# A hybrid encoder step: the first RMSNorm's weights move into PSUM, its inputs go first in the queue, and GpSimd's first work is placed behind the 1/sqrt chain

## The chip, the cores and the metric

The kernel runs on one core of a Trainium2 chip. The time is device microseconds (us) of one execution; lower is better. The engines are TensorE (PE; its weight loads are listed apart as PEld), VectorE (DVE), ScalarE (ACT), GpSimd (POOL) and SyncE (SP), which issues most of the DMAs. SBUF is the on-chip working memory, PSUM the memory that TensorE writes, in banks of 128 partitions by 512 fp32 columns.

## The reference

One step of a one-layer encoder over 592 tokens (16 learned meta tokens, 512 prompt tokens, 64 sample tokens), width 1024, all in fp32. Only the beginning matters here:

```
def _rmsnorm(x, w):
    xf = x.astype(jnp.float32)
    y = xf * lax.rsqrt(jnp.mean(xf * xf, axis=-1, keepdims=True) + EPS)
    return (y * w.astype(jnp.float32)).astype(x.dtype)
...
    h = _rmsnorm(x, p["norm1"])
    proj = h @ p["w_in"]
```

`proj` is 9232 columns wide. What follows it is differential attention, a gated delta rule with a causal convolution, a gated merge, and a squared-ReLU MLP of hidden width 4096.

## The kernel before

TensorE multiplies in a reduced-precision fp32 format (fp32r), so every operand is split into a high and a low part and each product is three matmuls: high by high, low by high, high by low. The normed tokens `h` are kept transposed, features on partitions, as `hh` (high) and `hl` (low), 128 x 8 x 592. The projection weights stream in tasks of 256 columns. Each raw half (`wr_d`, 512 KB) is cast by ACT to `wh_d` and its rest is `wl_d`, for the first task always on POOL.

Python code writes all engines' instructions down in one fixed order. Two parts take turns: `begin`, which makes `hh` and `hl`, and the generator `main` (from `stream`), which loads and splits weights and issues the projection matmuls `pg_d`. Each `next(main)` in `begin` lets `main` go one step: first the loads of the first task's weights, then their split, then eight matmuls at a time.

`begin` works on five token tiles (80, 128, 128, 128, 128 rows), tokens on partitions. SP loads them as `x_s` (`load_x`), and loads `norm1` repeated over all 128 partitions as `n_bc`. For a tile t:

- `square(t)`: ACT squares the row and sums it (`jk`, a READ_ACCUMULATOR follows). For tiles 0 to 2 POOL meanwhile makes `xn` = x times `n_bc`.
- `rsqrt`: nine tiny DVE instructions (`rsv`, `rsy`, `rst`, 128 x 3) give 1/sqrt for tiles 0 to 2 at once, and later, 128 x 2, for tiles 3 and 4.
- `scale(t)`: DVE multiplies by it (tiles 3 and 4: by it and by `n_bc`).
- `turn(t)`: TensorE transposes `xn` in two halves of four 128-column blocks into PSUM banks `pxt`; ACT casts each half to `hh`, and DVE subtracts to give `hl` (both in `split`).

The projection's columns are worked in two parts: tokens 0 to 335, which need tiles 0 to 2, and tokens 336 to 591, which need tiles 3 and 4 too. Five PSUM banks are shared by everything that asks `bank` for one.

DVE, ACT, POOL and TensorE each take their instructions strictly in this written order.

Of the kernel before, what the change touches and what calls it, by code (L numbers as in the profile page):

```python
# [208 lines left out]
def stream_step_kernel(  # L209
# [243 lines left out]

    def load_x(pl, t, nm):
        xt = pl.tile([P, D], F32, name=f"x_{nm}{t}", tag="xt")
        if t == 0:
            Q.dma_start(xt[0:16], meta)
            Q.dma_start(xt[16:80], x_prompt[0, 0:64])
        elif t < 4:
            Q.dma_start(xt, x_prompt[0, 128 * t - 64:128 * t + 64])  # L460
        else:
            Q.dma_start(xt[0:64], x_prompt[0, 448:512])
            Q.dma_start(xt[64:128], x_sample[0])
        return xt

    def begin(sp):

        n1_bc = sp.tile([P, D], F32, name="n1_bc", tag="n1")
        ss = sp.tile([P, NT], F32, name="ss", tag="ss")
        v1 = sp.tile([P, P], F32, name="v1", tag="v1")  # L470
        v2 = sp.tile([P, P], F32, name="v2", tag="v2")
        V.memset(ss, 1.0)
        S.activation(ss[:, 4:5], ss[:, 4:5], AF.Square)
        xts = [load_x(sp, t, "s") for t in range(2)]
        Q.dma_start(n1_bc, flat(norm1, 0, [[0, P], [1, D]]))
        Q.dma_start(ident, consts[:, 0:P])
# [9 lines left out]
        Q.dma_start(v2[74:75].rearrange("o (a d) -> o a d", a=2), flat(q_norm, 0, [[64, 1], [0, 2], [1, 64]]))  # L486
        Q.dma_start(cst[:, P:3 * P], consts[:, P:3 * P])
        xns = {}

        def square(t):  # L490
            n = TILES[t][1]
            jk = sp.tile([P, D], F32, name=f"jk{t}", tag="jk")
            S.activation(jk[:n], xts[t][:n], AF.Square, accum_out=ss[:n, t:t + 1])
            xns[t] = sp.tile([P, D], F32, name=f"xn{t}", tag="xn")
            if t < 3:
                G.tensor_tensor(xns[t][:n], xts[t][:n], n1_bc[:n], ALU.mult)

        def scale(t, r):
            n = TILES[t][1]
            if t < 3:  # L500
                V.tensor_scalar(xns[t][:n], xns[t][:n], r[:n], None, ALU.mult)
            else:
                V.scalar_tensor_tensor(xns[t][:n], xts[t][:n], r[:n], n1_bc[:n], ALU.mult, ALU.mult)

        def turn(t):
            c0, n = TILES[t]
            for q in range(2):
                pv = bank(f"pxt{t}{q}").rearrange("p (k c) -> p k c", k=4)
                for k in range(4):
                    TE.transpose(pv[:, k, :n], xns[t][:n, (4 * q + k) * P:(4 * q + k + 1) * P], ident[:n, :n])  # L510
                split(hh[:, 4 * q:4 * q + 4, c0:c0 + n], hl[:, 4 * q:4 * q + 4, c0:c0 + n], pv[:, :, :n])

        for t in range(3):
            square(t)
        r = rsqrt(sp, ss[:, 0:3], 3, 1.0 / D, EPS)
        for t in range(3):
            scale(t, r[:, t:t + 1])
        next(main)
        square(3)
        turn(0)  # L520
        turn(1)
# [29 lines left out]
    def prepare(sp):  # L551
# [1013 lines left out]
```

## Time and profile before

| | |
|---|---|
| runs of the kernel before | 1348.81 us median of 3 (1346.97 to 1351.1) |
| the profiled execution | 1348.32 us, of which the profile's span is 1346.5 us |
| TensorE busy | 1297.8 us (96% of the span) |
| VectorE busy | 694.0 us (52%) |
| ScalarE busy | 564.5 us (42%) |
| GpSimd busy | 264.7 us (20%) |
| mean granted TensorE clock | 0.994 |

The times in the trace count from the start of the span. A busy share is over the whole span; the stretch of interest is its first 40 us, where the shares are quite different.

### The profile page before, as it was taken

The numbers are of one execution on the slowest core, as the hardware profiler recorded it, in microseconds if no ns is written. First come the engines' busy times: TensorE is split into PE (matmuls) and PEld (weight loads), VectorE is DVE, ScalarE is ACT, GpSimd is POOL, SyncE is SP. The second block draws the span as 40 slices with busy tenths as digits, with TensorE's granted clock in tenths as the row PEclk, the third lists the DMA queues.
The fourth block names the chain that finished last, engine by engine and source line by source line (L and its number), as shares of the span: only waits on it lengthen the run. The fifth ranks groups of instructions, "written<-read, shape, count | busy, mean of one in ns | idle before, by whom it ended". The sixth has DMA issues, their size and how long they took to land.

```text
span 1346.5 us, 25748 instructions
## 1 busy us (share of the span) xinstructions
PE 1297.8 (96%) x10365; PEld 1260.4 (94%) x10365; DVE 694.0 (52%) x1547; ACT 564.5 (42%) x1354; POOL 264.7 (20%) x283
## 2 busy tenths in 40 slices
PE   2999999999999999999899999999999999999998
PEld 2998899999899999998788899999999999999998
DVE  5766899533457624448877844445333233233232
ACT  3556544343563343346676723233431431431421
POOL 5101412200132000062524102100410410310300
PEclk9999999999999999999999899999999999999999
DMA  6313343532644422685644256622223223222231
GB/s 174 90 53 116 100 124 113 169 91 72 196 135 127 141 78 66 189 242 162 198 141 135 94 203 226 204 78 80 79 79 95 76 82 94 67 92 86 72 112 53
DMA packets 163947, 161.07 MB, mean 120 GB/s; under 512 B 23546, under 2 KB 143628, under 8 KB 163828
## 3 DMA queue, kind: packets, MB, share of 16 engines
q1 hardware_dynamic: 162372, 155.99, 38.2%
q0 software_dynamic: 1456, 3.44, 0.9%
q8 instruction: 81, 1.33, 0.4%
q14 instruction: 38, 0.31, 0.1%
HBM read 124.46 MB, written 37.88 MB: 121 GB/s over the span
## 4 chain that ended last, share of the span: by engine, by line
PE 46%; DVE 3%; DMA 1%; ACT 1%; issue 0%; SPq 0%; DVEq 0%; ACTq 0%
PE pg_dn L164 15%; PE pg_u L164 15%; PE pg_o L164 4%; PE pg_bb L164 4%; PE pg_ba L164 3%; PE pg_g L164 1%; DVE sc L164 1%; PE ppo L164 1%; DVE mx L164 1%; PE psc L164 1%; PE pwT L164 1%; ACT sc L164 0%; DMA thb<-th_d 0%; PE pxr L164 0%; PE pyo L164 0%
## 5 line engine op out<-in xcount | busy, mean ns | idle before, releaser
L164 PE MATMUL pg_dn<-uh,wh_dn 128*128 128x288 f32 x512 | 151.6, 296 | 0.0
L164 PE MATMUL pg_dn<-ul,wh_dn 128*128 128x288 f32 x512 | 151.6, 296 | 0.0
L164 PE MATMUL pg_u<-h2h,wh_u 128*128 128x288 f32 x512 | 151.4, 296 | 0.0
L164 PE MATMUL pg_u<-h2h,wl_u 128*128 128x288 f32 x512 | 151.2, 295 | 0.0
L164 PE MATMUL pg_u<-h2l,wh_u 128*128 128x288 f32 x512 | 151.2, 295 | 0.0
L164 PE MATMUL pg_dn<-uh,wl_dn 128*128 128x288 f32 x512 | 151.1, 295 | 0.0
L164 PE MATMUL pg_a<-wh_a,hh 128*128 128x256 f32 (+1 forms) x480 | 136.3, 284 | 2.0 <-ACT sq L164 2.0
L164 PE MATMUL pg_a<-wh_a,hl 128*128 128x256 f32 (+1 forms) x480 | 136.3, 284 | 0.0
L164 PE MATMUL pg_a<-wl_a,hh 128*128 128x256 f32 (+1 forms) x480 | 135.4, 282 | 0.0
L164 PE MATMUL pg_d<-hl,wh_d 128*128 128x336 f32 (+1 forms) x384 | 116.1, 302 | 0.6 <-DVE hl L164 0.6
L164 PE MATMUL pg_d<-hh,wh_d 128*128 128x336 f32 (+1 forms) x384 | 116.0, 302 | 0.6 <-ACT hh L164 0.6
L164 PE MATMUL pg_d<-hh,wl_d 128*128 128x336 f32 (+1 forms) x384 | 115.8, 302 | 0.0
L164 POOL TENSOR_TENSOR wl_u<-wr_u,wh_u 128x1024 fp32r<-128x1024 f32 x22 | 52.9, 2402 | 260.5 <-ACT wh_u L164 260.5
L164 DVE TENSOR_TENSOR x<-x,pg_dn 128x288 f32<-128x288 f32 x64 | 29.1, 454 | 132.5 <-PE pg_dn L164 132.5
L164 PEld LDWEIGHTS pg_u<-h2h,wh_u 128*128 128x128 f32 x512 | 96.5, 189 | 0.1
L164 PEld LDWEIGHTS pg_u<-h2l,wh_u 128*128 128x128 f32 x512 | 96.5, 189 | 0.0
L164 PEld LDWEIGHTS pg_u<-h2h,wl_u 128*128 128x128 f32 x512 | 96.4, 188 | 0.0
L164 PEld LDWEIGHTS pg_dn<-uh,wl_dn 128*128 128x128 f32 x512 | 96.3, 188 | 0.0
L164 PEld LDWEIGHTS pg_dn<-ul,wh_dn 128*128 128x128 f32 x512 | 96.1, 188 | 0.0
L164 PEld LDWEIGHTS pg_dn<-uh,wh_dn 128*128 128x128 f32 x512 | 96.1, 188 | 0.0
L164 PEld LDWEIGHTS pg_a<-wh_a,hh 128*128 128x128 f32 (+1 forms) x480 | 86.5, 180 | 3.1 <-ACT sq L164 2.5
L164 PEld LDWEIGHTS pg_a<-wh_a,hl 128*128 128x128 f32 (+1 forms) x480 | 86.7, 181 | 0.7 <-issue 0.6
(371 smaller groups left out, 3536.6 us busy)
## 6 DMA issues: line engine op xcount, KB each, us to landing
wr_u<-in_w_up_dram SPq DMA_DIRECT2D x32, 512.0 KB, 3.6
wr_dn<-in_w_down_dram SPq DMA_DIRECT2D x32, 512.0 KB, 3.5
wr_d<-in_w_in_dram SPq DMA_DIRECT2D x24, 512.0 KB, 3.9
wr_a<-in_w_in_dram SPq DMA_DIRECT2D x24, 512.0 KB, 4.1
wr_g<-in_w_in_dram SPq DMA_DIRECT2D x16, 512.0 KB, 5.5
at_d<-st SPq DMA_DIRECT2D x48, 128.0 KB, 2.2
th_d<-gt SPq DMA_DIRECT2D x16, 288.0 KB, 2.2
wr_z<-in_w_in_dram SPq DMA_DIRECT2D x8, 512.0 KB, 3.8
```

The costliest lines, as they stand in the source:

```text
L164: r = f(*a, **kw)
```

## The change

All of it lies in `begin` and in one line of `prepare`.

- `norm1` is loaded as one row of 1024 and spread over the partitions by two matmuls of a row of ones with it, into two PSUM banks (`pn10`, `pn11`; `pn` in a profile). These banks stay taken until the last `scale`.
- Tokens go first in SP's queue: tiles 0, 1, 2, then the row, then the identity.
- POOL's multiplications by `norm1` are gone. `scale` does both products in DVE, in two instructions of 512 columns, for all five tiles.
- POOL's first instruction now is a tiny copy that reads the result of the 1/sqrt chain. The split of the first weights (`wl_d`) is queued behind it.
- `turn` leaves the `hl` subtractions to a new function `lower`, which `begin` calls after the next tile's `scale`. Tile 3's squares on ACT move behind the casts of tile 2, and tiles 3 and 4 are transposed after 24 and 32 matmuls.
- The ones come from a DVE memset at the start, not from POOL's in `prepare`.

```diff
-    def load_x(pl, t, nm):
+    def load_x(pl, t):
...
-        n1_bc = sp.tile([P, D], F32, name="n1_bc", tag="n1")
+        n1 = sp.tile([1, D], F32, name="n1", tag="n1")
...
+        xts = [load_x(sp, t) for t in range(3)]
+        Q.dma_start(n1, norm1)
+        Q.dma_start(ident, consts[:, 0:P])
         V.memset(ss, 1.0)
+        V.memset(onesr.bitcast(F32), 1.0)
         S.activation(ss[:, 4:5], ss[:, 4:5], AF.Square)
-        xts = [load_x(sp, t, "s") for t in range(2)]
-        Q.dma_start(n1_bc, flat(norm1, 0, [[0, P], [1, D]]))
-        Q.dma_start(ident, consts[:, 0:P])
-        xts.append(load_x(sp, 2, "s"))
         next(main)
...
+        n1_bc = [bank(f"pn1{q}") for q in range(2)]
+        for q in range(2):
+            TE.matmul(n1_bc[q], onesr.bitcast(F32)[0:1, :], n1[:, 512 * q:512 * q + 512], start=True, stop=True)
...
-            xns[t] = sp.tile([P, D], F32, name=f"xn{t}", tag="xn")
-            if t < 3:
-                G.tensor_tensor(xns[t][:n], xts[t][:n], n1_bc[:n], ALU.mult)
 
         def scale(t, r):
             n = TILES[t][1]
-            if t < 3:
-                V.tensor_scalar(xns[t][:n], xns[t][:n], r[:n], None, ALU.mult)
-            else:
-                V.scalar_tensor_tensor(xns[t][:n], xts[t][:n], r[:n], n1_bc[:n], ALU.mult, ALU.mult)
+            xns[t] = sp.tile([P, D], F32, name=f"xn{t}", tag="xn")
+            for q in range(2):
+                cs = slice(512 * q, 512 * q + 512)
+                V.scalar_tensor_tensor(xns[t][:n, cs], xts[t][:n, cs], r[:n], n1_bc[q][:n], ALU.mult, ALU.mult)
...
-                split(hh[:, 4 * q:4 * q + 4, c0:c0 + n], hl[:, 4 * q:4 * q + 4, c0:c0 + n], pv[:, :, :n])
+                hi, lo = (x[:, 4 * q:4 * q + 4, c0:c0 + n] for x in (hh, hl))
+                S.copy(hi, pv[:, :, :n])
+                rest.append((lo, pv[:, :, :n], hi.bitcast(F32)))
+            return rest
+
+        def lower(rest):
+            for lo, pv, hi in rest:
+                V.tensor_tensor(lo, pv, hi, ALU.subtract)
...
-        for t in range(3):
-            scale(t, r[:, t:t + 1])
+
+        G.tensor_scalar(ss[:, 0:3], r, 1.0, 0.0, ALU.mult, ALU.add)
         next(main)
+        scale(0, r[:, 0:1])
+        rest = turn(0)
+        scale(1, r[:, 1:2])
+        lower(rest)
+        rest = turn(1)
+        scale(2, r[:, 2:3])
+        lower(rest)
+        rest = turn(2)
         square(3)
-        turn(0)
-        turn(1)
         square(4)
-        turn(2)
+        lower(rest)
...
-            if i in (3, 5):
-                turn(3 if i == 3 else 4)
+            if i in (2, 3):
+                lower(turn(i + 1))
...
-        G.memset(onesr.bitcast(F32), 1.0)
```

GpSimd's queue from its first instruction on, before (`xn` is the product with `norm1`, `wl_d` the low part of the first weights):

```order
L164 TENSOR_TENSOR xn0_196<-x_s0_168,n1_bc_162 80x1024
L164 TENSOR_TENSOR xn1_200<-x_s1_171,n1_bc_162 128x1024
L164 TENSOR_TENSOR xn2_204<-x_s2_175,n1_bc_162 128x1024
L164 TENSOR_TENSOR wl_d010_222<-wr_d0100_177,wh_d010_221 128x1024
L164 TENSOR_TENSOR wl_d010_222<-wr_d0104_179,wh_d010_221 128x1024
L164 DMA ba_r_382<-in_w_in_dram 128x8x16
```

and with the change:

```order
L164 TENSOR_SCALAR ss_163<-rsy3_207 128x3
L164 TENSOR_TENSOR wl_d010_219<-wr_d0100_178,wh_d010_218 128x1024
L164 TENSOR_TENSOR wl_d010_219<-wr_d0104_180,wh_d010_218 128x1024
L164 DMA ba_r_390<-in_w_in_dram 128x8x16
```

The three products are gone, and the two weight splits stand behind an instruction that needs `rsy`, the last result of the 1/sqrt chain.

VectorE's queue from the end of that chain on, before (`hl` the low part of the transposed tokens, its last operand the cast `hh`):

```order
L164 SCALAR_TENSOR_TENSOR rsy3_208<-rst2_207,rsy3_208 128x3
L164 TENSOR_SCALAR xn0_196<-xn0_196,rsy3_208 80x1024
L164 TENSOR_SCALAR xn1_200<-xn1_200,rsy3_208 128x1024
L164 TENSOR_SCALAR xn2_204<-xn2_204,rsy3_208 128x1024
L164 TENSOR_TENSOR hl_158<-pxt00_230,hh_157 128x4x80
```

and with the change, up to the first subtraction that the second matmul needs:

```order
L164 SCALAR_TENSOR_TENSOR xn0_224<-x_s0_166,rsy3_207,pn10_195 80x512
L164 SCALAR_TENSOR_TENSOR xn0_224<-x_s0_166,rsy3_207,pn11_196 80x512
L164 SCALAR_TENSOR_TENSOR xn1_239<-x_s1_169,rsy3_207,pn10_195 128x512
L164 SCALAR_TENSOR_TENSOR xn1_239<-x_s1_169,rsy3_207,pn11_196 128x512
L164 TENSOR_TENSOR hl_158<-pxt00_227,hh_157 128x4x80
L164 TENSOR_TENSOR hl_158<-pxt01_233,hh_157 128x4x80
L164 SCALAR_TENSOR_TENSOR xn2_256<-x_s2_171,rsy3_207,pn10_195 128x512
L164 SCALAR_TENSOR_TENSOR xn2_256<-x_s2_171,rsy3_207,pn11_196 128x512
L164 TENSOR_TENSOR hl_158<-pxt10_244,hh_157 128x4x128
L164 TENSOR_TENSOR hl_158<-pxt11_250,hh_157 128x4x128
L164 TENSOR_TENSOR hl_158<-pxt20_261,hh_157 128x4x128
```

Tile 2 is now scaled behind tile 0's two subtractions, and tile 2's own first subtraction stands behind tile 1's.

On TensorE, where tile 3 is transposed, before (the 32nd matmul stands ahead of it; `pg_d01010` is the second output of the first task):

```order
L164 MATMUL pg_d01010_318<-hl_158,wh_d010_221 128x336
L164 MATMUL pxt30_327<-cst_74,xn3_229 128x128 x4
L164 MATMUL pxt31_334<-cst_74,xn3_229 128x128 x4
L164 MATMUL pg_d01010_318<-hh_157,wl_d010_222 128x336
```

and with the change (the 24th matmul ahead of it, and tile 4 eight matmuls later):

```order
L164 MATMUL pg_d01000_283<-hh_157,wl_d010_219 128x336
L164 MATMUL pxt30_326<-cst_74,xn3_304 128x128 x4
L164 MATMUL pxt31_332<-cst_74,xn3_304 128x128 x4
L164 MATMUL pg_d01010_340<-hh_157,wh_d010_218 128x336
```

Tile 3's transposes moved forward past eight matmuls. From the second column part on, the order on all five engines is the one of before, row for row, except for tile numbers.

## Rows read from the trace of the kernel before

**Rows 1.** The page, part 1: busy time by engine.
```profile
PE 1297.8 (96%) x10365; PEld 1260.4 (94%) x10365; DVE 694.0 (52%) x1547; ACT 564.5 (42%) x1354; POOL 264.7 (20%) x283
```

**Rows 2.** Waits of TensorE: us in total, times, longest.
```profile
PE pxt L164 <- DVE xn L164: 22.7, 1, 22.7
...
PE pkn L164 <- DVE ktok L164: 2.5, 1, 2.5
```

**Rows 3.** Timeline of ScalarE, 0 to 40 us: start, duration, what, [idle before].
```profile
10.73 1.06 ACT L164 ACTIVATE jk<-x_s 128x1024 f32<-128x1024 f32 x1 [3.49 <-DMA x_s<-in_x_prompt_dram]
...
12.13 1.04 ACT L164 CAST wh_d<-wr_d 128x1024 fp32r<-128x1024 f32 x1 [0.25 <-DMA wr_d<-in_w_in_dram]
14.70 1.05 ACT L164 CAST wh_d<-wr_d 128x1024 fp32r<-128x1024 f32 x1 [1.53 <-DMA wr_d<-in_w_in_dram]
...
27.33 1.06 ACT L164 CAST hh<-pxt 128x512 fp32r<-128x512 f32 x2
```

**Rows 4.** Timeline of VectorE, 8 to 31 us.
```profile
11.91 2.08 DVE L164 TENSOR_SCALAR rsv<-ss 128x3 f32<-128x3 f32 x1 [11.04 <-ACT jk L164]
...
18.62 2.21 DVE L164 TENSOR_TENSOR rst<-rst,rsy 128x3 f32<-128x3 f32 x1
...
21.91 2.08 DVE L164 TENSOR_SCALAR xn<-xn,rsy 80x1024 f32<-80x1024 f32 x3
24.01 1.02 DVE L164 TENSOR_TENSOR hl<-pxt,hh 128x320 fp32r<-128x320 f32 x2
...
27.93 1.29 DVE L164 TENSOR_TENSOR hl<-pxt,hh 128x512 fp32r<-128x512 f32 x2 [0.83 <-ACT hh L164]
29.14 0.16 DVE L164 TENSOR_SCALAR rsv<-ss 128x2 f32<-128x2 f32 x1
...
30.71 0.16 DVE L164 SCALAR_TENSOR_TENSOR rsy<-rst,rsy 128x2 f32<-128x2 f32 x1
```

**Rows 5.** Timeline of GpSimd, its first work.
```profile
9.27 6.94 POOL L164 TENSOR_TENSOR xn<-x_s,n_bc 80x1024 f32<-80x1024 f32 x3 [8.82 <-DMA n_bc<-in_norm_dram]
16.17 4.64 POOL L164 TENSOR_TENSOR wl_d<-wr_d,wh_d 128x1024 fp32r<-128x1024 f32 x2
```

**Rows 6.** Timeline of TensorE, 22 to 40 us.
```profile
22.72 4.66 PE L164 MATMUL pxt<-cst,xn 80*128 80x80 f32 x24 [22.72 <-DVE xn L164]
27.95 0.42 PE L164 MATMUL pg_d<-hh,wh_d 128*128 128x336 f32 x1 [0.57 <-ACT hh L164]
28.68 0.42 PE L164 MATMUL pg_d<-hl,wh_d 128*128 128x336 f32 x1 [0.31 <-DVE hl L164]
...
33.56 1.04 PE L164 MATMUL pxt<-cst,xn 128*128 128x128 f32 x8
...
38.17 0.39 PE L164 MATMUL pg_d<-hh,wh_d 128*128 128x256 f32 x1
38.90 0.39 PE L164 MATMUL pg_d<-hl,wh_d 128*128 128x256 f32 x1 [0.34 <-DVE hl L164]
```

**Rows 7.** A GpSimd tensor_tensor in the timeline at 622.66 us.
```profile
622.66 2.39 POOL L164 TENSOR_TENSOR wl_g<-wr_g,wh_g 128x1024 fp32r<-128x1024 f32 x1
```

**Rows 8.** Groups by shape, VectorE, 622.6 to 625.2, then 400 to 800: busy us, mean ns.
```profile
L164 DVE SCALAR_TENSOR_TENSOR aqT<-ptq,vec,aqT 128x464 fp32r<-128x464 f32 x1 | 0.7, 700 | 2.5 <-ACT aqT L164 2.5
...
L164 DVE SCALAR_TENSOR_TENSOR aqT<-ptq,vec,aqT 128x464 fp32r<-128x464 f32 x8 | 5.6, 696 | 5.8 <-ACT aqT L164 5.8
```

**Rows 9.** Timeline of TensorE, 105 to 112 us.
```profile
105.32 0.82 PE L164 MATMUL pk<-cst,kT 128*128 128x128 f32 x4 [1.35 <-DVE ktok L164]
...
108.22 0.48 PE L164 MATMUL pg_d<-hh,wh_d 128*128 128x336 f32 x1
108.50 0.48 PE L164 MATMUL pg_d<-hl,wh_d 128*128 128x336 f32 x1
...
111.52 0.77 PE L164 MATMUL pbv<-oh,rb 32*8 32x360 f32 x2
```

**Rows 10.** Busy us by engine in a stretch, then granted clock, DMA share, GB/s.
```profile
105.60:109.10 3.50, 3.44 (x16) 3.05 (x15) 1.68 (x3) 3.25 (x21) 0.00 (x0) 0.51 0.32 114
```

More of the change, by code (lines that the diff above doesn't have):

```diff
@@ L452, in stream_step_kernel @@
     ob = [x[:, :, 0:TQ] for x in (hh, hl)]
-    def load_x(pl, t, nm):
-        xt = pl.tile([P, D], F32, name=f"x_{nm}{t}", tag="xt")
+    def load_x(pl, t):
+        xt = pl.tile([P, D], F32, name=f"x_s{t}", tag="xt")
         if t == 0:
@@ L471, in begin @@
         v2 = sp.tile([P, P], F32, name="v2", tag="v2")
+        xts = [load_x(sp, t) for t in range(3)]
+        Q.dma_start(n1, norm1)
+        Q.dma_start(ident, consts[:, 0:P])
         V.memset(ss, 1.0)
+        V.memset(onesr.bitcast(F32), 1.0)
         S.activation(ss[:, 4:5], ss[:, 4:5], AF.Square)
-        xts = [load_x(sp, t, "s") for t in range(2)]
-        Q.dma_start(n1_bc, flat(norm1, 0, [[0, P], [1, D]]))
-        Q.dma_start(ident, consts[:, 0:P])
-        xts.append(load_x(sp, 2, "s"))
         next(main)
-        xts += [load_x(sp, t, "s") for t in range(3, NT)]
+        xts += [load_x(sp, t) for t in range(3, NT)]
         Q.dma_start(v1[0:96], conv_w[0].rearrange("w (c p) -> (w c) p", p=P))
@@ L493, in square @@
             S.activation(jk[:n], xts[t][:n], AF.Square, accum_out=ss[:n, t:t + 1])
-            xns[t] = sp.tile([P, D], F32, name=f"xn{t}", tag="xn")
-            if t < 3:
-                G.tensor_tensor(xns[t][:n], xts[t][:n], n1_bc[:n], ALU.mult)
         def scale(t, r):
             n = TILES[t][1]
-            if t < 3:
-                V.tensor_scalar(xns[t][:n], xns[t][:n], r[:n], None, ALU.mult)
-            else:
-                V.scalar_tensor_tensor(xns[t][:n], xts[t][:n], r[:n], n1_bc[:n], ALU.mult, ALU.mult)
+            xns[t] = sp.tile([P, D], F32, name=f"xn{t}", tag="xn")
+            for q in range(2):
+                cs = slice(512 * q, 512 * q + 512)
+                V.scalar_tensor_tensor(xns[t][:n, cs], xts[t][:n, cs], r[:n], n1_bc[q][:n], ALU.mult, ALU.mult)
         def turn(t):
             c0, n = TILES[t]
+            rest = []
             for q in range(2):
@@ L527, in begin @@
                 r = rsqrt(sp, ss[:, 3:5], 2, 1.0 / D, EPS)
-                for t in range(2):
-                    scale(3 + t, r[:, t:t + 1])
-            if i in (3, 5):
-                turn(3 if i == 3 else 4)
+                scale(3, r[:, 0:1])
+                scale(4, r[:, 1:2])
+            if i in (2, 3):
+                lower(turn(i + 1))
         ps = bank("pv1")
```

## The prediction

> **What bounds the kernel now.** First the busy times: TensorE is busy 96% of the span [rows 1], so only its idle time and its own work can be removed. Its list of waits comes second: the longest by far, 22.7 us, is the one before the first transposes, for `xn` [rows 2]; every later one is at most 2.5 us. So I read the first 40 us engine by engine. There the reader should follow one chain. Tile 2's square starts at 10.73, when its tokens have landed [rows 3]; the 1/sqrt chain starts at 11.91 and its last instruction is over only just before `scale` starts at 21.91 [rows 4]. Nine instructions take ten us. The same nine for tiles 3 and 4 run from 29.14 to 30.87 (30.71 and 0.16), 1.73 us [rows 4]. The difference is in the first four, which take 2.08 to 2.26 us (the first and the fourth are shown), though they handle three columns. GpSimd's five instructions run without a gap from 9.27 to 20.81 [rows 5], 2.3 us each, the length of the slow DVE rows; the fourth slow row ends at 20.83, with GpSimd's last. I read it as DVE waiting for one GpSimd instruction each time.
>
> Behind it come `scale`, 24 transposes, casts and subtractions; the first projection matmul starts at 27.95, the second, which needs `hl`, at 28.68 [rows 6]. From there TensorE nearly streams.
>
> **The change step by step.** I time the new beginning on the scale of the trace.
>
> *Tokens.* Tile 2 takes the queue place of the repeated `norm1`, which had landed when POOL began at 9.27 [rows 5]. I put tile 2 at 9.2. It could be as late as 10.73, where it is now, or as early as 8.1: 512 KB fewer are ahead of it, and such a piece takes 1.4 to 2.6 us (10.73 to 12.13, 12.13 to 14.70 [rows 3]). From its square to the chain's start passes 1.18 us (10.73 to 11.91), so the chain runs from 10.4 to 12.1 if no GpSimd instruction stands against it: 1.73 us instead of 9.9. POOL has none to run until the chain ends.
>
> *norm1 in PSUM.* Not seen in the trace. Nearest is an fp32 matmul with 360 columns, whose two records take 0.77 us [rows 9]. For 512 columns that is 1.1 us, so 2.2 for both matmuls at full clock and 4.4 at half. With the row landing by 9.0 the second bank is ready between 11.2 and 13.4; `scale` wants it at 12.8, the first at 12.1. It costs 0 to 0.6 us, and I take 0.1; the cover is the 1/sqrt chain, and each us that the row lands later costs up to one us.
>
> *Scale.* Two DVE instructions a tile. The nearest row has the same three operands (PSUM, a scalar per partition, SBUF) with 464 columns: 0.70 us [rows 8]; back to back, 512-column instructions reading PSUM come every 0.645 (1.29 for two [rows 4]). I take 0.66, so 1.32 a tile, where before it was 0.69 (2.08 for three). This is 1.9 us more on DVE for three tiles.
>
> *The weights' casts.* ACT casts the second half of the first weights before it casts any `hh`. That half landed at 14.70 [rows 3]. With 512 KB less ahead, 1.4 to 2.6 us as above, I take 1.4: 13.3, and the cast is over at 14.35. Ends: 12.1 and 14.7.
>
> *The chain to the second matmul.* Tiles 0 and 1 are scaled by 12.1 + 2.64 = 14.74. The first `hh` cast takes 0.48 from 14.35, so the first subtraction starts at about 14.86. Then DVE alone sets the pace, in the order that the listing above shows: tile 0's subtractions 1.02, tile 2's scale 1.32, tile 1's subtractions 1.25, tile 2's first 0.69 [rows 4]: 19.14. The second matmul starts at 19.2, against 28.68: 9.5 us earlier. The transposes and casts between lie beside this. Three banks are left to `pxt`, so tile 1's second half waits for tile 0's first subtraction and tile 2's second half for tile 1's; at half clock (24 transposes in 4.66, so 0.8 for four [rows 6]) the last one ends near 18.8, before it is needed.
>
> *The weights' low part.* POOL starts at 12.2 instead of 16.17, and needs 4.64 [rows 5]: by 17.0, as the second cast allows it to start at 14.4. Cover 2.2 us.
>
> *Tile 3's new place, a new wait.* TensorE reaches its transposes after 24 matmuls. From 28.68 to 33.56 there are 31 steps, 0.157 us each [rows 6]; 23 more of them end at 22.8. But ACT now squares tiles 3 and 4 after the casts of tile 2 (those end near 19.5): 2 x 1.15 us, then the chain 1.73, then half a scale 0.70: 24.3. TensorE waits 1.5 us. What stands behind it: the 24 remaining matmuls of the part and tile 4. From the transposes to the second column part it was 33.56 to 38.17, 4.61 us with 16 matmuls; with 24 it is 5.87, so 30.2, and 0.2 to 0.4 for the second half of the scale and the next matmul: 30.6 against 38.90, where the trace also had a wait for `hl` [rows 6]. That `hl` is over by 29.5 now. **Gain there: 38.9 - 30.6 = 8.3 us.**
>
> From here all queues hold the same rows as before. The later waits of TensorE are for DVE and ACT work that itself follows matmuls, so they move along. With the 0.1 for `norm1` I keep 8.2 us. The profiled execution took 1348.32 us, so 1340.1; the median of the runs shown stands 0.5 higher, and I predict 1340.4. About 0.3% (4 us) is what a measurement of this kernel can tell from no change, as its three runs lie 4.1 apart.
>
> **The rivals.**
>
> *TensorE stays at half clock.* Now its work before the first projection matmul is 24 transposes in one go, at 0.19 us each against 0.13 later [rows 6], and the matmuls behind run at full pace; after the change the transposes come in bursts of four with waits between, and the 1.5 us wait follows. The half level looks like [rows 10]: granted 0.51 (1.2 GHz) from 105.6 to 109.1, matmuls 0.28 apart [rows 9]. If the first 24 matmuls ran so, they would take 24 x 0.12 = 2.9 us more, of which the wait at tile 3 hides 1.5; or the wait itself brings on one such stretch, 3.5 us at half, 1.7 lost. Gain 6.5 to 6.8: 1341.7. For it: the fall at 105.6 came right after a wait of 1.35 us [rows 9]. Against: the clock did not fall at 28, after 0.57 and 0.31 us [rows 6], and the 1.5 us wait is a single one. Chance 0.16.
> The Trainium skill speaks for this rival: in "TensorE: Matmul & The Clock Gate", section "HAM oscillation — how this bites in real kernels", it says that work in bursts with waits between them lets the array fall back to the low clock. By it the time would be this rival's 1341.7, by the rows at 28 us my own; the 3.5 us at 0.51 show that the fall exists here.
>
> *GpSimd blocks the new scales too.* If DVE's `scale` waited for the two `wl_d` instructions as the tiny ones did, tile 1's first half would be scaled only at 17.0; then 0.66 + 1.02 + 1.32 + 1.25 + 0.69 follow: 22.0 instead of 19.2. Gain 5.4: 1342.9. For it: the rows at 11.91 to 20.83. Against: while a GpSimd tensor_tensor ran from 622.66 to 625.05 [rows 7], the instruction with a PSUM operand, a scalar and an SBUF operand took 700 ns, against 696 in the mean of all eight [rows 8]. Chance 0.07.
>
> *The slow rows had another cause* (ACT, the DMAs of that time), so the chain still takes 9.9 us from 10.4. Then `scale` starts at 20.3, the second matmul at 27.2, and the wait at tile 3 takes back the 1.5: no change, 1348. Against: the slow rows end with GpSimd's last one to 0.02 us. Chance 0.03.
>
> *The gain is given back*, most likely where TensorE waits 2.5 us for `ktok` [rows 2]: if that wait were set by a transfer that starts at a fixed time, it would grow by what was gained. It is a DVE result, so against it. 1345 to 1348. Chance 0.06.
>
> *norm1's row lands late, and the kernel is slower.* It is a single small row behind 1.3 MB of tokens. Every us after about 9 delays both banks, `scale` and all behind it by one us. From a landing at 17.3 on the gain is gone, and past 21.3 the kernel is slower by over 0.3%: 1352.5 and more. Against: what stood in about the same place had landed at 9.27 [rows 5]. Chance 0.03.
>
> **How the numbers follow.** The forecast has the remaining 0.65. Its own bounds: tile 2 and the weights at their early ends give one us more, and at their late ends (10.73 and 14.70) 1.4 to 1.5 less (both start the same chain, so they don't add up); with the scatter of the runs 1338 to 1342.5. The range takes in the half clock and the blocked scales, 1337.5 to 1344.5; the last three rivals, 0.12, lie outside. Faster by over 0.3%: 0.65 + 0.16 + 0.07 = 0.88. Within 0.3%: 0.09. Slower: 0.03.
>
> **What would show it.** Right: nine DVE rows of 0.16 us, from about 10.4 to 12.1; tile 2's square at about 9.2; `scale` rows of 0.7 with GpSimd's `wl_d` beside them; the second cast of weights at 13.3; the second `pg_d` matmul near 19.2; a wait of about 1.5 us before tile 3's transposes; the first 256-column matmuls near 30.5, and later waits as long as now. Wrong: any `scale` row of over 2 us, a wait of `scale` for `pn`, projection matmuls 0.28 apart before 30 us, or waits after 40 us whose sum is some us greater than now.

## The result, and the profile after

The changed kernel takes 1337.43 us (median of 8 runs, 1334.18 to 1345.09), the kernel before beside it 1347.67 (8 runs, 1344.41 to 1352.61): ratio 0.9939, 95% interval 0.9920 to 0.9958, or 8.2 us less (the ratio is not that of the two medians, which lie 10.2 us apart). In a second set of runs it took 1338.32 us (8 runs), ratio 0.9949 (0.9927 to 0.9971). The forecast was 8.2 us less; applied to the 1348.81 of the runs that it had, the ratio gives 1340.6 beside 1340.4. The median itself lies 0.07 us under the range's low end; the eight runs of before have a median 1.1 us below that of the three shown, too.

The timeline of the profiled execution of the changed kernel, 7 to 30 us: VectorE, ScalarE, GpSimd, then TensorE (start, duration, engine, what, [idle before]).

```profile
9.68 0.17 DVE L164 TENSOR_SCALAR rsv<-ss 128x3 f32<-128x3 f32 x1 [8.65 <-ACT jk L164]
...
11.27 0.16 DVE L164 SCALAR_TENSOR_TENSOR rsy<-rst,rsy 128x3 f32<-128x3 f32 x1
11.54 2.72 DVE L164 SCALAR_TENSOR_TENSOR xn<-x_s,rsy,pn 80x512 f32<-80x512 f32 x4
14.18 0.88 DVE L164 TENSOR_TENSOR hl<-pxt,hh 128x320 fp32r<-128x320 f32 x2
14.98 1.39 DVE L164 SCALAR_TENSOR_TENSOR xn<-x_s,rsy,pn 128x512 f32<-128x512 f32 x2
16.29 2.00 DVE L164 TENSOR_TENSOR hl<-pxt,hh 128x512 fp32r<-128x512 f32 x3
...
8.50 1.06 ACT L164 ACTIVATE jk<-x_s 128x1024 f32<-128x1024 f32 x1 [1.26 <-DMA x_s<-in_x_prompt_dram]
...
11.68 1.05 ACT L164 CAST wh_d<-wr_d 128x1024 fp32r<-128x1024 f32 x1 [0.50 <-DMA wr_d<-in_w_in_dram]
...
11.61 0.20 POOL L164 TENSOR_SCALAR ss<-rsy 128x3 f32<-128x3 f32 x1 [11.16 <-DVE rsy L164]
11.77 4.69 POOL L164 TENSOR_TENSOR wl_d<-wr_d,wh_d 128x1024 fp32r<-128x1024 f32 x2
...
7.47 3.75 PE L164 MATMUL pn<-n,onesr 1*128 1x512 f32 x4 [7.47 <-DMA n<-in_norm_dram]
12.34 5.80 PE L164 MATMUL pxt<-cst,xn 80*128 80x80 f32 x24 [1.13 <-DVE xn L164]
17.80 0.63 PE L164 MATMUL pg_d<-hh,wh_d 128*128 128x336 f32 x1
18.35 0.65 PE L164 MATMUL pg_d<-hl,wh_d 128*128 128x336 f32 x1
18.79 0.48 PE L164 MATMUL pg_d<-hh,wl_d 128*128 128x336 f32 x1
...
19.60 0.32 PE L164 MATMUL pg_d<-hh,wl_d 128*128 128x336 f32 x1
...
23.56 1.29 PE L164 MATMUL pxt<-cst,xn 128*128 128x128 f32 x8 [0.87 <-DVE xn L164]
...
29.39 0.36 PE L164 MATMUL pg_d<-hh,wh_d 128*128 128x256 f32 x1
29.59 0.28 PE L164 MATMUL pg_d<-hl,wh_d 128*128 128x256 f32 x1
```

The chain's nine rows, of which the first and the last are shown, last 0.16 to 0.17 us each and end at 11.43; before, four of them took over 2 us [rows 4]. `wl_d` runs beside four `scale` rows that come 0.66 apart. From 11.54 to 18.29 the VectorE rows follow each other without a gap, and the second `pg_d` matmul starts at their end: 18.35, against 28.68 [rows 6]. The first five `pg_d` matmuls are still 0.28 apart, the half level that [rows 9, 10] show; from 19.6 on they come at 0.155. The second column part starts at 29.39, 8.8 us earlier, and its second matmul, without the old wait for `hl`, at 29.59, 9.3 us earlier.

What happens to these 9.3 us later is seen at three waits of TensorE, and in two of the stretches at half clock of that execution (busy us of TensorE, its weight loads, DVE, ACT, POOL with counts; then granted clock, DMA share, GB/s).

```profile
95.90 0.66 PE L164 MATMUL pk<-cst,kT 128*128 128x128 f32 x4 [1.35 <-DVE ktok L164]
...
132.62 0.50 PE L164 MATMUL pkn<-cst,ktok 80*128 80x80 f32 x4 [0.67 <-DVE ktok L164]
...
573.85 0.39 PE L164 MATMUL pg_a<-wh_a,hh 128*128 128x256 f32 x1 [1.23 <-ACT sq L164]
...
466.70:480.30 13.60, 13.60 (x114) 12.86 (x113) 0.98 (x2) 3.57 (x7) 0.00 (x0) 0.50 0.06 23
651.00:654.40 3.40, 3.40 (x18) 3.38 (x17) 2.06 (x10) 1.42 (x4) 0.16 (x1) 0.50 0.11 38
```

Two of these lines in the kernel before:

```profile
145.18 0.50 PE L164 MATMUL pkn<-cst,ktok 80*128 80x80 f32 x4 [2.48 <-DVE ktok L164]
...
581.74 0.39 PE L164 MATMUL pg_a<-wh_a,hh 128*128 128x256 f32 x1 [1.97 <-ACT sq L164]
```

At 95.90 the kernel is 9.4 us ahead of before [rows 9], and at the longest wait that before had behind its beginning, for `ktok` at 145.18, it is 12.6 us ahead, since that wait is 0.67 us instead of 2.48. At 573.85 it is 7.9 ahead, after 13.6 us at half clock where before had two stretches of 3.4 us (at 105.67 and 146.63). This execution, 1345.09 us, was the longest of the eight; its mean granted clock was 0.990, that of the three shortest 0.996 and 0.997. The waits of TensorE behind 40 us add up to some 20 us before, 21 in this execution and 17 in the one profiled the second time. The table sets the same marks beside each other for all kernels that ran; the wait for `ktok` is the one of the `pk` matmuls, the times are medians, the ratios stand against the runs of before on the same chip.

| kernel | first `scale` | 2nd `pg_d` | wait for `ktok` ends | time | ratio (95%) |
|---|---|---|---|---|---|
| before | 21.91 | 28.68 | 105.32 | 1347.67 | |
| changed | 11.54 | 18.35 | 95.90 | 1337.43 | 0.9939 (0.9920 to 0.9958) |
| changed, second time | 11.46 | 18.26 | 95.58 | 1338.32 | 0.9949 (0.9927 to 0.9971) |
| tokens first alone | 19.05 | 27.73 | 105.76 | 1346.78 | 1.0003 (0.9977 to 1.0029) |
| GpSimd kept busy | 17.24 | 24.05 | 101.58 | 1343.80 | 0.9976 (0.9964 to 0.9988) |
| `norm1` in SBUF | 11.06 | 21.18 | 98.57 | 1338.72 | 0.9954 (0.9932 to 0.9976) |
| no hold | 11.16 | 17.96 | 95.06 | 1337.77 | 0.9928 (0.9913 to 0.9942) |
| old order | 11.60 | 20.72 | 98.83 | 1338.42 | 0.9946 (0.9928 to 0.9964) |
| later turns | 11.30 | 18.10 | 95.74 | 1335.29 | 0.9925 (0.9902 to 0.9947) |
| early products | 11.83 | 18.24 | 94.08 | 1335.48 | 0.9927 (0.9903 to 0.9950) |
| early products, again | 10.67 | 16.96 | 92.93 | 1333.63 | 0.9908 (0.9887 to 0.9929) |
| early products, no hold | 11.34 | 19.73 | 96.01 | 1336.95 | 0.9933 (0.9913 to 0.9953) |
| later turns, dummies | 14.05 | 23.29 | 99.26 | 1340.87 | 0.9961 (0.9945 to 0.9977) |
| early products, dummies | 12.93 | 24.35 | 100.35 | 1341.39 | 0.9960 (0.9943 to 0.9978) |

The marks differ by some tenths from one execution to the next, the times by several us; the verdicts below rest on the marks, and on a time only where the interval allows it.

The record also has each run's span and mean granted clock. Their product is an estimate of the span at full clock throughout, which counts half of a stretch at half clock as lost; it scatters by up to 2 us (one standard deviation), the times by up to 5. By it the changed kernel of the second set is 10.3 us ahead of the 17 runs of before beside it (1327.9 against 1338.2), and in the same way later turns are 10.7 ahead, early products 12.0 and 11.4, no hold 8.8, early products without the hold 8.7, the old order 7.5, `norm1` in SBUF 6.9 and GpSimd kept busy 2.5, while tokens first alone are 0.4 behind. The granted clock itself was lower in the changed kernel, 0.9938 and 0.9931 in the mean of its two sets, than in the runs of before beside the second, 0.9958.

### The profile page after: what moved, and what is told of

It reads as the page before. It is cut to its first block, busy times and chain, and to the rows that moved or that the text cites. A ratio compares the mean times of both kernels' runs of the same rounds, so it can differ in the third digit from the quotient of the medians.

```text
span 1343.3 us, 25764 instructions
## 1 busy us (share of the span) xinstructions
PE 1307.8 (97%) x10369; PEld 1265.8 (94%) x10369; DVE 688.4 (51%) x1553; ACT 564.3 (42%) x1354; POOL 256.3 (19%) x280
## 4 chain that ended last, share of the span: by engine, by line
PE 84%; DVE 6%; DMA 5%; ACT 3%; issue 2%; SPq 1%; POOL 0%; DVEq 0%; ACTq 0%; POOLq 0%
PE pg_dn L164 15%; PE pg_u L164 15%; PE pg_a L164 10%; PE pg_d L164 8%; PE pg_g L164 6%; PE pg_z L164 4%; PE pg_ba L164 4%; PE pg_o L164 4%; PE pg_bb L164 4%; DVE sc L164 2%; DMA bias_d<-bv_d 2%; PE ppo L164 2%; PE po L164 1%; DVE mx L164 1%; PE psc L164 1%
```

## The experiments

### Is it GpSimd that made the chain slow?

**Tokens first alone.** The kernel before with one edit:

```diff
-        xts = [load_x(sp, t, "s") for t in range(2)]
+        xts = [load_x(sp, t, "s") for t in range(3)]
         Q.dma_start(n1_bc, flat(norm1, 0, [[0, P], [1, D]]))
         Q.dma_start(ident, consts[:, 0:P])
-        xts.append(load_x(sp, 2, "s"))
```

> The kernel before with one part of the change alone: tile 2's tokens go ahead of the repeated norm1 and the identity in SP's queue. GpSimd keeps its three products with norm1. Theory (GpSimd blocks the chain): tile 2's square is about 1.5 to 2 us earlier (8.5 to 9.3 instead of 10.73), but the products start when norm1 has landed, at 9.5 to 11, and run seven us, so that four or more of the chain's rows still take 2.1 to 2.3 us; the second pg_d matmul is at 27 to 29 against 28.68; total within 1.5 us of before. Rival (the gain of the change comes from the earlier tokens): the chain is short or starts early enough that the second matmul comes at 19 to 25, and the total falls by 4 us or more.

Its timeline, VectorE and GpSimd:

```profile
9.48 0.16 DVE L164 SCALAR_TENSOR_TENSOR rst<-rst 128x3 f32<-128x3 f32 x1
9.67 2.36 DVE L164 SCALAR_TENSOR_TENSOR rsy<-rst,rsy 128x3 f32<-128x3 f32 x1
12.07 2.27 DVE L164 SCALAR_TENSOR_TENSOR rst<-rsy,rsv 128x3 f32<-128x3 f32 x1
14.38 2.27 DVE L164 TENSOR_TENSOR rst<-rst,rsy 128x3 f32<-128x3 f32 x1
...
19.05 3.99 DVE L164 TENSOR_SCALAR xn<-xn,rsy 80x1024 f32<-80x1024 f32 x3
...
9.63 6.94 POOL L164 TENSOR_TENSOR xn<-x_s,n_bc 80x1024 f32<-80x1024 f32 x3 [9.18 <-DMA n_bc<-in_norm_dram]
```

This is the plainest view of the cause: five rows run at 0.16 to 0.17 before GpSimd starts at 9.63, and from the first that starts behind it on every row takes one GpSimd instruction (6.94 / 3 = 2.3 us). Tokens that are 3.2 us earlier (square at 7.50 instead of 10.73) win 0.95 us at the second matmul and nothing in the time.

**GpSimd kept busy.** The changed kernel, plus six products that nothing uses:

```diff
         xns = {}
+        spare = [sp.tile([P, D], F32, name=f"sq{t}", tag="spare") for t in range(1)][0]
...
             S.activation(jk[:n], xts[t][:n], AF.Square, accum_out=ss[:n, t:t + 1])
+            for _ in range((1, 1, 4, 0, 0)[t]):
+                G.tensor_tensor(spare[:n], xts[t][:n], xts[t][:n], ALU.mult)
```

> The changed kernel with one thing added that nothing uses: six products x times x of 1024 columns on GpSimd (tiles 0, 1 and four times 2, into a spare tile), ahead of its hold, so that GpSimd runs tensor_tensors from about 5 to 19 us as it did before, while tokens, norm1 in PSUM and all else stay as changed. Theory: the 1/sqrt chain again has about four rows of 2.1 to 2.3 us, ends at 18 to 20.5 instead of 11.43, and the second pg_d matmul is at 25 to 27.5 instead of 18.35: most of the 8.2 us gain is gone. Rival (the gain came from the order of the loads or from norm1 in PSUM): nine rows of 0.17, the chain ends at 11.4 to 12, the second matmul at 18.3 to 19.5, total within 1.5 us of the changed kernel (wl_d later, which the second matmul does not need).

```profile
10.85 0.17 DVE L164 TENSOR_SCALAR rsy<-rsv 128x3 int32<-128x3 int32 x1
11.06 1.73 DVE L164 SCALAR_TENSOR_TENSOR rst<-rsy,rsv 128x3 f32<-128x3 f32 x1
12.83 0.16 DVE L164 TENSOR_TENSOR rst<-rst,rsy 128x3 f32<-128x3 f32 x1
13.02 1.74 DVE L164 SCALAR_TENSOR_TENSOR rst<-rst 128x3 f32<-128x3 f32 x1
...
4.97 11.75 POOL L164 TENSOR_TENSOR sq<-x_s 80x1024 f32<-80x1024 f32 x6 [4.52 <-DMA x_s<-in_x_prompt_dram]
```

In this timeline (VectorE, then GpSimd) the slow rows are back with the tokens, `norm1` and the order as changed: four of 1.19 to 1.74 us. The second matmul is at 24.05, 5.7 us later than in the changed kernel, and its median is 6.0 us above that of the kernel named no hold below, which has the changed kernel's marks, on the same chip. I had expected 25 to 27.5: the GpSimd instructions took less than 2 us here (1.89 each, six in 11.75), and two rows of the chain, not one, passed per instruction. These instructions stand 0.08 us apart, those of the kernel before overlap by 0.04; whether that is why was not tried.

### What the place of norm1, the hold and the order are worth

**`norm1` in SBUF.** The changed kernel with these lines, and without the two matmuls:

```diff
-        n1 = sp.tile([1, D], F32, name="n1", tag="n1")
+        n1 = sp.tile([P, D], F32, name="n1", tag="n1")
...
-        Q.dma_start(n1, norm1)
+        Q.dma_start(n1, flat(norm1, 0, [[0, P], [1, D]]))
...
+        n1_bc = [n1[:, 512 * q:512 * q + 512] for q in range(2)]
```

> The changed kernel with norm1 not in PSUM: the DMA repeats it over the partitions of an SBUF tile at the same queue place (512 KB instead of 4 KB), `scale` reads x and norm1 both from SBUF, and the two norm1 matmuls are gone; the hold stays. Theory (blocking by GpSimd depends on where DVE's operands lie): `scale` rows now stand against the two wl_d (2.4 us each): one or two of the `scale` rows take 2 us or more instead of 0.73, or wl_d's own rows become longer, and the second pg_d matmul is at 20.5 to 22 instead of 18.35; total 2 to 3.5 us slower. Rival (PSUM does not matter for `scale`, only the chain's tiny rows were blocked): `scale` rows stay at 0.66 to 0.75, and the one cost is that norm1 and the weights land later by 1.2 to 2.6 us; `scale` starts as norm1 lands, the second matmul is at 18.3 to 20; total 0 to 1.5 us slower.

Timeline of VectorE and GpSimd:

```profile
11.06 2.74 DVE L164 SCALAR_TENSOR_TENSOR xn<-x_s,rsy,n 80x512 f32<-80x512 f32 x4
14.24 0.89 DVE L164 TENSOR_TENSOR hl<-pxt,hh 128x320 fp32r<-128x320 f32 x2 [0.44 <-ACT hh L164]
15.05 4.27 DVE L164 SCALAR_TENSOR_TENSOR xn<-x_s,rsy,n 128x512 f32<-128x512 f32 x2
...
12.48 6.29 POOL L164 TENSOR_TENSOR wl_d<-wr_d,wh_d 128x1024 fp32r<-128x1024 f32 x2 [0.53 <-ACT wh_d L164]
```

Tile 2's two rows take 4.27 us (1.52 and 2.83) instead of 1.39, and the two `wl_d` 6.29 instead of 4.69: the first one had started while tile 1's rows ran, and was itself held up. The second matmul moves from 18.35 to 21.18, as the theory had it. The rival, a later landing, falls: tile 2's rows start at 15.05, against 14.98, so the loss is in the rows themselves. The time is less plain: the ratio is 0.9954 against 0.9928 for no hold on the same chip, 3.5 us with intervals that overlap, while the medians lie 1.0 apart and the estimates at full clock 1.8. So PSUM is what lets `scale` run beside GpSimd.

**No hold.** The changed kernel without its line `G.tensor_scalar(ss[:, 0:3], r, 1.0, 0.0, ALU.mult, ALU.add)`.

> The changed kernel without GpSimd's tiny first instruction, so that its two wl_d may start as soon as the first cast of the weights is over (11.18 us in the trace of the changed kernel), while the 1/sqrt chain runs from 9.68 to 11.43. Theory (a DVE instruction with all operands in SBUF waits for the GpSimd tensor_tensor that is running): the last one or two rows of the chain take up to 2.3 us instead of 0.17, `scale` starts at 13 to 16 instead of 11.54, and the second pg_d matmul is at 19.8 to 22.5 instead of 18.35; total 1.5 to 4 us slower. Rival (the slow rows had another cause, and the hold does nothing): nine rows of 0.17, `scale` at 11.5, the second matmul at 18.3 to 18.5, no difference in time.

The rival's numbers came, though not for its reason: `wl_d` waits for the first cast of the weights and starts at 10.88, and of the chain only the last row, at 10.89, was still to come. It took 0.16, although a row that started 0.04 us behind a GpSimd instruction took 2.36 in tokens first alone; why this one escaped is not shown. Behind it `scale` has its PSUM operand. Here the hold is worth nothing (from the first `scale` to the second matmul pass 6.8 us with and without it); the landing of the weights holds GpSimd as long. Where that cover is gone, it is worth something, as early products without the hold shows in the next part.

**Old order.** The changed kernel with the instructions behind the chain in the order of before, the subtractions back in `turn`:

```diff
+        for t in range(3):
+            scale(t, r[:, t:t + 1])
+        square(3)
+        turn(0)
+        turn(1)
+        square(4)
+        turn(2)
...
-            if i in (2, 3):
-                lower(turn(i + 1))
+            if i in (3, 5):
+                turn(3 if i == 3 else 4)
```

> The changed kernel with one part undone: the order of the kernel before for DVE, ACT and TensorE behind the chain (all three `scale`, tile 3's square, then the transposes of tiles 0, 1 and 2 each with its casts and subtractions, tile 4's square ahead of tile 2's; tiles 3 and 4 transposed after 32 and 48 matmuls). The chain, norm1 in PSUM, the queue and the hold stay as changed. Theory (the most of the gain is the chain's; the new order is worth its share because the squares of tiles 3 and 4 stand ahead of casts that the second matmul needs, and wait for their tokens): the chain ends at 11.0 to 11.5, the second pg_d matmul is at 20 to 22.5 instead of 18.35, and there is no wait before tile 3's transposes; the first 256-column matmul is at 30 to 32; total 0.5 to 2.5 us slower than the changed kernel. Rival (the order matters little, VectorE's sum of work alone sets the second matmul): it is at 18.3 to 19.2, and the total is the same or, without the wait at tile 3, up to 0.9 us less.

Timeline of ScalarE, VectorE and TensorE:

```profile
14.64 1.06 ACT L164 ACTIVATE jk<-x_s 128x1024 f32<-128x1024 f32 x1 [1.30 <-DMA x_s<-in_x_prompt_dram]
...
15.70 1.22 ACT L164 CAST hh<-pxt 128x320 fp32r<-128x320 f32 x3
...
12.61 3.38 DVE L164 SCALAR_TENSOR_TENSOR xn<-x_s,rsy,pn 80x512 f32<-80x512 f32 x5 [0.27 <-PE pn L164]
...
8.83 3.75 PE L164 MATMUL pn<-n,onesr 1*128 1x512 f32 x4 [8.83 <-DMA n<-in_norm_dram]
```

The first `hh` cast stands behind tile 3's square, which waits for its tokens until 14.64; the second matmul is at 20.72, and the wait for `ktok` ends 3 us later than in the changed kernel (12 matmuls at half clock, until it rose at 24.10, are in this; the changed kernel had five). The median does not show it (1338.42, against 1338.32 on the same chip): 3 us at this mark are no more than the later half-clock stretches differ between executions. The estimate at full clock does, 7.5 us ahead of before instead of 10.3. In this execution the row of `norm1` also landed 1.4 us later, and `scale` waited 0.27 us for its second bank.

**The changed kernel a second time.**

> The changed kernel once more, unaltered, as the measure for the kernels beside it. Theory (its profiled execution of 1345.1 us was longer than its others because of two stretches at half clock, 13.65 us at 466.68 and 3.41 us at 651.00, which have nothing to do with the beginning): the first 30 us are the same to 0.5 us (second pg_d matmul at 18 to 18.5), the pk matmuls stand at 95 to 96 again, and the time is 1335 to 1339. Rival (the new beginning itself brings the stretches on): the 13.65 us at half clock near 467 are there again, and the median is above 1340.

The marks came again (18.26, 95.58), the 13.6 us at half clock did not; at the wait for `sq` it stood at 569.07, 12.7 us ahead of before. So the change does not bring that stretch each time; the lower mean clock of its two sets leaves open whether it brings such stretches more often.

### What is left at the beginning

**Later turns.** The changed kernel with `if i in (3, 4): lower(turn(i))`: tiles 3 and 4 are transposed eight matmuls later.

> The changed kernel with tiles 3 and 4 transposed after 32 and 40 projection matmuls instead of 24 and 32. Theory (the wait at tile 3 is an idle time of TensorE that the change need not have): the 0.87 us wait before tile 3's transposes is gone or below 0.2, the second pg_d matmul stays at 18.3, the first 256-column matmul is at 28.4 to 28.9 instead of 29.39, and the total falls by 0.5 to 1 us, less than the scatter of the times. Rival (the wait covers something that is late next, tile 4's casts or subtractions): as much idle time appears before the second column part, and the first 256-column matmul stays at 29.2 to 29.6.

Timeline of TensorE:

```profile
18.10 0.65 PE L164 MATMUL pg_d<-hl,wh_d 128*128 128x336 f32 x1
18.55 0.48 PE L164 MATMUL pg_d<-hh,wl_d 128*128 128x336 f32 x1
...
24.89 1.04 PE L164 MATMUL pxt<-cst,xn 128*128 128x128 f32 x8
...
29.23 0.36 PE L164 MATMUL pg_d<-hh,wh_d 128*128 128x256 f32 x1
```

The wait at tile 3 is gone, and still the second column part starts at 29.23 (29.39 and 29.08 in the changed kernel). The rival's number came, but not for its reason: no wait took the place of the one removed. Here the clock rose only at 22.33, and some 15 matmuls ran 0.28 apart. The wait and the half clock roughly stand in for each other: in the changed kernel the wait was 1.18 us with the clock up at 17.44 (second time), and 0.87 with the clock up at 19.53.

**Early products.** Later turns, and besides:

```diff
+        Q.dma_start(n1, norm1)
         xts = [load_x(sp, t) for t in range(3)]
-        Q.dma_start(n1, norm1)
...
+        def early(t):
+            n = TILES[t][1]
+            xns[t] = sp.tile([P, D], F32, name=f"xn{t}", tag="xn")
+            for q in range(2):
+                cs = slice(512 * q, 512 * q + 512)
+                V.tensor_tensor(xns[t][:n, cs], xts[t][:n, cs], n1_bc[q][:n], ALU.mult)
...
+            if t < 2:
+                V.tensor_scalar(xns[t][:n], xns[t][:n], r[:n], None, ALU.mult)
+                return
...
+        early(0)
+        early(1)
         r = rsqrt(sp, ss[:, 0:3], 3, 1.0 / D, EPS)
...
-        G.tensor_scalar(ss[:, 0:3], r, 1.0, 0.0, ALU.mult, ALU.add)
+        scale(0, r[:, 0:1])
+        scale(1, r[:, 1:2])
+        G.tensor_scalar(ss[:, 0:3], xns[1][:, 0:3], 1.0, 0.0, ALU.mult, ALU.add)
         next(main)
-        scale(0, r[:, 0:1])
         rest = turn(0)
-        scale(1, r[:, 1:2])
```

> A kernel made from what the profile after shows, VectorE busy without a gap from the chain's end to the second matmul: norm1's row goes first in the queue, VectorE multiplies tiles 0 and 1 by it while it waits for tile 2's tokens, so that behind the chain these tiles need one 1024-column instruction with SBUF operands each (0.7 us) instead of two with PSUM (1.36); GpSimd is held until both are scaled; tiles 3 and 4 are transposed after 32 and 40 matmuls. Theory: the products lie in time in which VectorE has nothing else, the chain ends at 11.4 to 12, the two tiles are scaled 0.8 to 1.1 us earlier than now (at 13.2), the second pg_d matmul is at 17.2 to 17.9 instead of 18.35, the first 256-column matmul at 27.4 to 28.3 instead of 29.39; total 1 to 2 us less than the changed kernel. Rival (norm1 in PSUM is ready too late at half clock, and the products run into the chain): the chain starts late by as much as is saved, the second matmul is at 18.2 to 19, and only the wait at tile 3 is gone.

> The kernel with the early products, the later transposes and the hold behind both scales, once more and unaltered, as the measure for the one beside it. Theory: the second pg_d matmul at 18.0 to 18.5, the first 256-column matmul at 27.4 to 29 (28.5 or more if the clock rises only at 20 us or later), 1334 to 1337 us. Rival (its first time of 1335.5 was luck of the half-clock stretches): the median is at 1337 to 1340, as that of the changed kernel.

The products were over at 8.1 us, ahead of the chain in both runs. In the first, tile 2's tokens came late (square at 8.87) and the second matmul was at 18.24, as the rival said, for another reason; in the second (square at 7.71) it was at 16.96 and the second column part at 26.43. The median is 1335.48 us, beside 1338.32 for the changed kernel on the same chip (all five runs 1334.57 to 1337.55, its eight 1336.69 to 1341.36), and 1333.63 on another one. It has the lowest median here; by the two pairs of ratios, 0.9927 and 0.9908 against 0.9939 and 0.9949, some 3 to 4 us faster than the change, with intervals that in part overlap. How much of that is the later turns alone is open: these had 0.9925. At the marks the later turns do show here: the second column part follows the second matmul after 9.35 and 9.47 us, against 11.04 and 10.82 in the changed kernel, since there is no wait at tile 3 and the clock was up before the second matmul (at 16.86 and 15.31).

**Early products, no hold.** The same without the line `G.tensor_scalar(...)`.

> The kernel with the early products and the later transposes, without GpSimd's hold, so that nothing but the first cast of the weights (over at 11.54) keeps GpSimd from its wl_d, while the chain (10.05 to 11.79) and the two scales that have all operands in SBUF (11.83 to 13.24) are still to come. Theory (GpSimd's running tensor_tensor makes a DVE instruction with SBUF operands wait): wl_d starts at 11.5 to 11.7, the last row of the chain or the first scale is over only at 13.8 to 14, the second wl_d follows at 13.9 and may hold the second scale up to 16.3; the first transposes start at 14 to 14.5 instead of 12.63, the second pg_d matmul is at 19.5 to 21.5 instead of 18.24, and the total is 1 to 3 us more than that of the kernel with the hold. Rival (the hold does nothing, as in the changed kernel): rows of 0.17 and scales of 0.7, the second pg_d matmul at 18.0 to 18.5, no difference.

Timeline of VectorE and GpSimd:

```profile
11.14 0.16 DVE L164 SCALAR_TENSOR_TENSOR rsy<-rst,rsy 128x3 f32<-128x3 f32 x1
11.34 3.39 DVE L164 TENSOR_SCALAR xn<-xn,rsy 80x1024 f32<-80x1024 f32 x2
...
11.15 5.80 POOL L164 TENSOR_TENSOR wl_d<-wr_d,wh_d 128x1024 fp32r<-128x1024 f32 x2 [10.70 <-ACT wh_d L164]
```

The two scales, with SBUF operands again, take 3.39 us instead of 1.41, and the second matmul is at 19.73 although the chain was 0.5 us earlier than in the first run with the hold. From the first `scale` to the second matmul pass 8.4 us, against 6.4 and 6.3 with the hold: it is worth some 2 us at that mark where it has something to protect. The times, 1336.95 beside 1333.63 us on the same chip, point the same way with intervals that overlap.

**Dummies.** Unused matmuls in TensorE's idle time, to have the clock up in time; 50 ahead of the `norm1` matmuls and 10 behind them on later turns, 20 and 45 on early products:

```diff
+        wm = bank("pwarm")
+        for _ in range(50):
+            TE.matmul(wm[:, 0:P], onesr, onesr, start=True, stop=True)
...
+        for _ in range(10):
+            TE.matmul(wm[:, 0:P], onesr, onesr, start=True, stop=True)
```

> The kernel with the later transposes (tiles 3 and 4 after 32 and 40 matmuls) and 60 unused 128x128 matmuls of ones by ones more: 50 ahead of the norm1 matmuls and 10 between these and the first transposes, while TensorE has nothing else. Theory (what is left of TensorE's loss ahead of 30 us is its half clock: norm1's matmuls 3.75 us for four records, the 24 transposes at 0.2 each, and in the kernel without the 60 the first 15 pg_d matmuls at 0.28 instead of 0.155, until the granted clock rose at 22.33): the clock is at 1.0 before the first pg_d matmul, norm1's matmuls take about 1.9 us, the second pg_d matmul stays near 18.1 since VectorE sets it, all pg_d matmuls come every 0.155 us, tile 3's transposes wait again for up to 1.2 us (the half clock had hidden that), and the first 256-column matmul is at 28.2 to 28.8 instead of 29.23; total the same to 1 us less. Rival (such matmuls don't count, or the later bursts and waits let the clock fall again): matmuls 0.28 apart up to 20 us or later, the first 256-column matmul at 29 to 30.

> The kernel with the early products and the later transposes, with 65 unused 128x128 matmuls of ones by ones more: 20 ahead of the norm1 matmuls and 45 behind them, ahead of the first transposes. Theory (with the early products it is TensorE at half clock, 4.95 us for 24 transposes, that makes the last casts late, and VectorE waits for a cast at 13.9): the transposes take 3.2 to 4.2 us, the first pg_d matmul is at 16.3 to 17 instead of 17.51 and the second at 17.0 to 17.7 instead of 18.24, every one of them at 0.155; then tile 3's transposes may wait up to 0.5 us; the first 256-column matmul is at 26.6 to 27.4 instead of 27.59; total 0 to 1 us less. Rival (the casts and VectorE's own order set it, not the clock): the second matmul stays at 18.1 to 18.4, and the first 256-column matmul at 27.4 to 27.8.

Timeline of TensorE in the first of the two:

```profile
1.09 10.93 PE L164 MATMUL pwarm<-onesr 128*128 128x128 f32 x50 [1.09 <-DVE onesr L164]
11.95 3.78 PE L164 MATMUL pn<-n,onesr 1*128 1x512 f32 x4
15.65 2.40 PE L164 MATMUL pwarm<-onesr 128*128 128x128 f32 x10
17.85 4.02 PE L164 MATMUL pxt<-cst,xn 80*128 80x80 f32 x20
```

Both failed. A dummy took 0.22 us, so the first 50 lasted until 12 us, and in this kernel the `norm1` matmuls came 4.5 us and the transposes 5.8 us later than in later turns. And the clock did not come up: the 20 transposes behind them still took 0.20 us each, and the record of the granted clock begins at 21.59. The second matmul is 5 and 6 to 7 us later than in the same kernels without dummies. Whether other data or longer rows would have raised it was not tried.

## Why the prediction was right, point by point

- **Tokens.** Tile 2's square at 8.50, inside 8.1 to 10.73 and 0.7 earlier than the 9.2 taken; 7.50 to 8.87 in the other kernels' traces.
- **The chain.** Forecast 10.4 to 12.1, nine rows of 0.16; it ran from 9.68 to 11.43. That GpSimd's running instruction is what a row waits for was argued from one coincidence of 0.02 us; tokens first alone and GpSimd kept busy show it, and the rival of another cause falls.
- **`norm1`.** The row landed at 7.47 and the four records took 3.75 us, the half-clock end of the range (4.4); the second bank was ready at 11.2, ahead of the chain. Cost 0 instead of 0.1. The rival that it lands late showed itself once, with 0.27 us.
- **Scale.** 0.66 apart, as taken, with `wl_d` at 2.36 beside it. The rival of blocked scales was held unlikely for the right reason, the PSUM operand: with it in SBUF tile 2's rows took 1.52 and 2.83 us. The Trainium skill says so too, in "SBUF — State Buffer", section "Who interferes with whom": a DVE instruction with two SBUF inputs contends with a GpSimd instruction that reads SBUF, one with at most one such input does not unless it runs in a mode that uses both ports, which a tensor_scalar can, and who issues first holds the other up for the whole instruction. The traces agree: the chain's tensor_scalar rows were held up too (2.08 us [rows 4]), `scale` with its PSUM operand was not, and `wl_d` took 3.54 us where it had started behind a `scale` from SBUF.
- **The weights' casts** are the one step outside its bounds: the second started at 11.68, not 13.3 (12.1 to 14.7). I took 1.4 us for 512 KB less ahead of it, and it landed 3 us earlier. So no subtraction had to wait for the weights, and the step was mis-sized by 1.6 us.
- **The second matmul** came at 18.35, not 19.2: 0.7 earlier from the chain and the cast; VectorE sets it, as forecast, but only just: tile 2's first subtraction starts at 17.60, 0.03 us after the cast that it reads is over (16.98 + 0.59), so the path of transposes and casts, which I had put beside this, is as long. `wl_d` was over at 16.46 (17.0).
- **The wait at tile 3** was 0.87 us, not 1.5. Most of the difference is the half clock of the first five `pg_d` matmuls (5 x 0.125 = 0.6 us); with the clock up earlier, the second time, it was 1.18, still 0.3 short. One sign that I had named as showing me wrong, matmuls 0.28 apart before 30 us, did come: the rival's mechanism was there, in a shorter stretch, and the wait hid it, as the rival's working had it in part; the later-turns kernel shows the exchange from the other side. The rule named with that rival, bursts and waits that let the clock fall, did not show: once up at 19.53 it stayed up through the 0.87 us wait and the 1.35 us one at 95.90, to 466.68. What came was a late rise. The section of the Trainium skill that I had named for this rival tells of longer waits than these, so it spoke for it less than I made of it.
- **The sum.** 9.3 us at the second 256-column matmul instead of 8.3, of which 0.85 stands at the second matmul already. That it would be kept held for the waits: the `pk` matmuls' wait for `ktok` ends 9.4 us earlier, the 2.5 us one that the rival named shrank to 0.67 us and to none the second time, and the waits behind 40 us add up to some 21 and 17 us instead of 20. At the end 8.2 us are measured (0.9939) and 6.9 the second time (0.9949 of 1344.77), 1 to 2.5 us less than the beginning gives, but no more than the intervals allow. The estimate at full clock has 10.3 us in the second set, so what is missing there goes with the granted clock, 0.9931 against 0.9958 (0.0027 x 1340 = 3.6 us). Whether the change lowers it or chance did is not shown; no hold, later turns and the old order, whose beginnings differ little, have 0.9952 to 0.9956. That forecast and measurement both read 8.2 is luck: the beginning gave 1 us more than the sum, and the interval spans 5.7 to 10.8. The sum's last step has a slip as well, since 1340.1 and the 0.5 that it adds make 1340.6, not 1340.4.

## What to carry over

Look first at small VectorE instructions that last as long as the GpSimd instruction beside them; what helps is to give GpSimd its work after the chain, or to let VectorE read one operand from PSUM. The hold cost nothing here, but a hold is worth something only where nothing else holds the engine already: look for what its queue waits for anyway. An order that puts work with a late input ahead of a cast on a strict queue can undo 2 us of such a gain without the median showing it.

## What the runs showed of the hardware

- VectorE and GpSimd block each other both ways: rows of 0.16 us took 2.3 (where GpSimd's instructions stood 0.08 us apart, every second row passed in 0.16), and `wl_d` of 2.36 us took 3.47 and 3.54 while VectorE's SBUF rows ran.
- TensorE ran through 16.7 us of matmuls of ones and `norm1` without a pause and was then still at the half level (transposes of 0.20 us); the rise came 3.7 us after the transposes had begun. In the thirteen traces beside before it came 3.1 to 13.0 us after the first transpose, and the 15 matmuls at 0.28 in one of them cost 15 x 0.125 = 1.9 us.
- Ahead of its first record the profile gives a granted clock of 1.00, whatever the matmuls' spacing says; there, the level is read from the spacing (0.28 against 0.155).
- A stretch at half clock of 13.6 us began at 466.68 with TensorE busy without a gap; no other of the traces has it, though one with dummies has 10.2 us at 270.76.
